# All GpSimd sums and products of a hybrid DeltaNet and pooling step issued on VectorE, with a new port rule in the kernel's scheduler

## The chip, the cores and the metric

The kernel runs on one core of one Trainium2 chip. The metric is the device time of one execution in microseconds. Before the change it is 2344.27 us, the median of three runs (2341.98 to 2349.40).

The core has five instruction queues that run beside each other, each in its own order: TensorE (PE in the profile; its weight loads are PEld), VectorE (DVE), ScalarE (ACT), GpSimd (POOL) and SyncE (SP), which issues the DMA transfers here. An instruction waits at the head of its queue until the semaphores of the instructions it depends on have come; what stands behind it waits too.

## The reference

One layer on 2048 prompt frames and 64 frames of a running stream, model width 1024, in float32:

```
h    = rmsnorm(x, norm1_w);  proj = h @ w_in          # q, k, v, z (4 heads x 128 each), a, b, pooling input
q,k,v = silu(conv4(qkv));  q,k = l2norm(q), l2norm(k)
# per head, chunks of tokens:  Lm = strict_lower((k*beta) k^T * gamma);  T = (I + Lm)^-1
# u = T (v*beta), w = T (k*beta*exp(G));  S carried from chunk to chunk;  o = q S + (q k^T * gamma) v_new
o    = rmsnorm(o) * silu(z)
pool = (sum of the last 2/4/8/16 frames / count - frame) @ pool_w * pool_scale
x    = x + concat(o, pool) @ w_out
h    = rmsnorm(x, norm2_w)
x    = x + (silu(h @ w_gate) * (h @ w_up)) @ w_down   # inner width 2816
y    = rmsnorm(x, normf_w)
```

The outputs are y of both streams and the new convolution, delta and pooling states.

## The kernel before

**Precision.** A large matmul is three: a float32 factor is split into a high part (ScalarE copies it to the matmul type fp32r) and a low part (VectorE subtracts the copy from the original), and high x high, high x low and low x high are added in PSUM. So each weight tile and each activation tile costs one ScalarE copy and one VectorE subtraction (`wsplit`, line 571; `split`, line 711).

**First part, up to about 948 us.** Four token blocks (576, 512, 512 and 512 tokens). Per block: the norm (`norm_stats`, `norm_apply`), the input projection (matmuls `pp`), the convolution and SiLU, and for each of 16 block-heads two `Front`s of two chunks. A `Front` (line 908) inverts a triangular 128x128 matrix in seven doubling levels: at each level `Um`, which is `U` times a mask, then fp16 matmuls `py`, a ScalarE copy `Yt`, fp16 matmuls `pt`, and an update of `TV` by VectorE. `Head` then walks through the chunks with the carried state. `pool_group` (line 1281) makes the window sums by doubling (`pw`). The output projection has the matmuls `pz`. The front's matmuls run in fp16 or plain float32 between the projections' fp32r ones.

**Second part, from about 948 us.** Three token blocks of 704, each in two halves of 352. For each of 22 inner tiles, `gate_up` (line 1561) makes the gate and the up projection as a 2x2 block product with seven instead of eight products (Strassen's scheme in Winograd's form): the seven products go into three PSUM accumulators, called px, py and pz here, 84 matmuls of 128x352 in all. Between the products the hurried instructions `g`, `u` and `hr` read those accumulators: before the last product can be added to px, VectorE must have made `u<-px,u`, so TensorE waits for it there. The down projection does the same for most groups (`down_strassen`, matmuls dx, dy, dz) and is plain for the rest (`down`, matmuls d). The sums and differences that the scheme needs are made of the weights (`prep_strassen`, line 624, tiles wr and wrS; `prep_down`, line 658, tiles wrdt, wrdl, wrda, wrdb) and of the activations (`factors`, line 1622, tiles q and hr; `stats2`, line 1356, tiles xt and xd). The gate and up weights are prepared in the first of the three blocks, stored, and mostly read back in the later ones.

**What sets the order.** The kernel first notes all operations in program order (`Machine.note`), and then plays them on a model of the five engines (`Machine.play`, line 237): each operation has a cost (`cost`, line 141), an occupancy `occ` of its engine and a latency `lat`, and each engine takes the ready operation of the lowest rank. Two plays are made; after the first, `deadlines` turns TensorE's order into due times, which are the ranks of the other engines in the second. The order of the second play is the order in which every queue is issued. All instructions are issued at line 206, so every row of the profile has that line; rows are told apart by tile names.

Around the change: the model knows that VectorE and GpSimd get in each other's way. An operation with `port` set is lengthened by what the other engine's last one still has to run, by no more than its own occupancy (line 361). GpSimd's operations all have it, VectorE's only with two inputs of the output's shape and none in PSUM. Operations that go to GpSimd before the change: the four sums of `prep_strassen` and of `prep_down`, the four of `factors` and of `stats2`, the running sums of squares of the norms (`rstd`, `last_norm`), the product in `norm_apply`, the `Um`, `Umf`, `Gst` operations and one `TV` of each `Front`, the pooling sums, the product with silu(z) in `Head.norm`, and the low parts of four of eight activation tiles in `load_h` (table `HPOOL`) - beside 193 small copies (2 to 15 elements a partition) and some memsets.

Of the kernel before, what the change touches and what calls it, by code (L numbers as in the profile page):

```python
# [19 lines left out]
P = 128  # L20
# [39 lines left out]
class Machine:  # L60
# [80 lines left out]
    def cost(self, op, name, out, ins):  # L141

        n = 1
        for d in out.shape[1:]:
            n *= d
        if op.eng == "tensor":
            dt = ins[0].dtype
            if name == "transpose":
                op.kind, op.ldw, op.occ = "f", 0.11, 0.109
            elif dt == F32:  # L150
                op.kind, op.ldw, op.occ = "f", 0.11, 0.012 + 1.651e-3 * n
            elif dt == F32R:
# [12 lines left out]
        if op.eng == "vector":
            op.lat = (0.215 if name == "scalar_tensor_tensor" else 0.15) + 1.045e-3 * n
            if name == "memset":
                op.lat = 0.14 + 0.5e-3 * n
            op.occ = op.lat - 0.083
            op.port = 1 if wide > 1 and not ps else 0  # L170
        elif op.eng == "scalar":
            op.lat = (0.16 if ps else 0.2) + 0.84e-3 * n + 0.095 * max(0, len(ins) - 1)
            op.occ = op.lat - 0.1
            if "accum_out" in op.call[2]:
                op.lat, op.occ = 0.6, 0.3
        else:
            op.port = 1
            if len(ins) > 1:
                op.lat = 0.05 + (2.45e-3 if n <= 512 else 1.92e-3) * n
            else:  # L180
                op.lat = 0.19 + 0.85e-3 * n
            op.occ = op.lat - 0.05

# [152 lines left out]
    def run(self, op, t):  # L336
        op.start = t
        if op.eng == "tensor":

            free, kind = self.free["tensor"], op.kind  # L340
            if self.last == kind and op.ready <= free:
                op.start = max(t, self.at + op.ldw)
            elif kind == "r":
                if op.ready <= free:
                    op.start = max(op.ready, free - (0.028 if self.last == "h" else 0.081))
                op.occ, op.lat = op.occ + 0.087, op.lat + 0.087
            elif self.last == "h":
                op.occ, op.lat = op.occ + 0.054, op.lat + 0.054
            else:
                op.occ, op.lat = op.occ + 0.02, op.lat + 0.02  # L350
            self.at, self.last = op.start, kind
            self.free["tensor"] = op.start + op.occ
        elif op.eng == "sync":
            self.free["sync"] = t + op.occ
            self.wire = max(self.wire, t + op.occ) + op.size / (400e3 if op.size > 300000 else 320e3)
            op.lat = self.wire + 1.35 - t
        else:
            if op.port:

                other = "gpsimd" if op.eng == "vector" else "vector"  # L360
                more = min(max(self.busy[other] - t, 0.0), op.occ)
                op.occ, op.lat = op.occ + more, op.lat + more
                self.busy[op.eng] = t + op.occ
            self.free[op.eng] = t + op.occ
# [31 lines left out]
def hybrid_kernel(ctx, tc, a, o):  # L396
# [173 lines left out]

    def wsplit(t, raw, n=512, eng=None):
        nc.scalar.copy(t[:, 0, :n], raw[:, :n])
        (eng or nc.vector).tensor_tensor(out=t[:, 1, :n], in0=raw[:, :n], in1=t[:, 0, :n].bitcast(F32), op=ALU.subtract)

    def prep():
# [31 lines left out]
        elif key[0] == "dn":  # L607
            _, m, f0, G = key
            raw, parts = (f() for f in wtiles("d", m % 2 == 0))
            nc.sync.dma_start(out=raw[:, : G * P], in_=a["wd"][m][:, f0 * P : (f0 + G) * P])  # L610
            wsplit(parts, raw, G * P, nc.vector)
        elif key[0] == "ds":
            parts = prep_down(*key[1:])
        else:
            parts = prep_strassen(key)
# [8 lines left out]
    def prep_strassen(key):  # L624
# [9 lines left out]
        if old:  # L634
            for i, nm in enumerate(FW):
                t[nm] = wtiles(nm, i % 2 == 1)[1]()
                if nm in gsd:
                    nc.sync.dma_start(out=flat(t[nm]), in_=gsd[nm][key[1]])
                else:
                    get(nm, nm)  # L640
                    wsplit(t[nm], raw[nm], 512, nc.vector)
            return t
        for nm, src in (("11", "11"), ("S1", "21"), ("22", "22"), ("12", "12")):
            get(nm, src)
        for nm in ("S3", "S2", "S4"):
            raw[nm] = wtiles(nm, True)[0]()
        gt = nc.gpsimd.tensor_tensor
        gt(out=raw["S3"], in0=raw["11"], in1=raw["S1"], op=ALU.subtract)
# [3 lines left out]
        for i, nm in enumerate(FW):  # L652
            t[nm] = wtiles(nm, i % 2 == 1)[1]()
            wsplit(t[nm], raw[nm], 512, nc.vector)
        due.append((key, [(gsd[nm][key[1]], t[nm]) for nm in FW if nm in gsd]))
        return t

    def prep_down(m, f0, G):
# [5 lines left out]
        s31, s24 = (wtiles(f"d{i}", True)[0]() for i in "ab")  # L664
        gt = nc.gpsimd.tensor_tensor
        left, right = slice(0, n), slice(n, 2 * n)
# [5 lines left out]
        for i, (nms, raw) in enumerate(((("11", "12"), top), (("S3", "S1"), s31), (("S2", "S4"), s24), (("22",), low[:, right]))):  # L672
            part = wtiles(f"d{nms[0]}", i % 2 == 1)[1]()
            wsplit(part, raw, n * len(nms), nc.vector)
            for j, nm in enumerate(nms):
# [86 lines left out]

    def rstd(tag, r, src, subs, pool, ttag, tbufs, eng):

        for lo, n in subs:
            rs = r[:, lo : lo + n]
            for k in range(KT):
# [3 lines left out]
                else:  # L771
                    sq = pool.tile([P, n], F32, tag=ttag, name=f"sq{k}{tag}{lo}", bufs=tbufs)
                    act(sq[:, :n], x, AF.Square)
                    eng.tensor_tensor(out=rs, in0=rs, in1=sq[:, :n], op=ALU.add)
                yield LAT_STAT
# [13 lines left out]
    def norm_stats(B):  # L789
# [8 lines left out]
        else:  # L798
            Chain(rstd(f"n1_{B.j}", B.r, stream_x(a["xT"], "xa", B.t0), [(0, B.NB)], gp, "ext", 4, nc.gpsimd))

    def norm_apply(B):
# [5 lines left out]
        for lo, n in S0 if B.j == 0 else [(0, B.NB)]:  # L807
            sl = slice(lo, lo + n)
            for k in range(KT):
# [5 lines left out]
                else:  # L815
                    t = src(k, lo, n)
                    nc.gpsimd.tensor_tensor(out=t, in0=t, in1=B.r[:, sl], op=ALU.mult)
                    act(h[:, 0, sl], t, AF.Copy, scale=w)
# [89 lines left out]
    class Front:  # L908
# [46 lines left out]
        def all(self):  # L955
# [42 lines left out]
            U = lev(F32, "Gst")  # L998
            nc.gpsimd.tensor_tensor(out=U, in0=Gam, in1=bc(ident, 2, C), op=ALU.subtract)
            yield LAT_G  # L1000
# [14 lines left out]
            for l in range(nlev):  # L1015
                Um = lev(F16, "Um", l, bufs=2)
                nc.gpsimd.tensor_tensor(out=Um, in0=U, in1=bc(lmask[:, l], 2, C), op=ALU.mult)
                py = self.ps(f"py{l}_{tag}")
                for c in range(2):
                    mm(py[:, c * C : (c + 1) * C], Um[:, c], id16 if l == 0 else TV[:, 0, c], start=True, stop=True)  # L1020
                if l == 0:
                    idb = bc(id16, 2, C)
                    TV = lev(F16, "TV", "", [P, 2, 2, C])
                    tt(TV[:, 0], idb, two(py), ALU.subtract)
                    nc.gpsimd.tensor_tensor(out=TV[:, 1], in0=idb, in1=Um, op=ALU.subtract)
                else:
# [16 lines left out]
            F0 = lev(F16, "Um", "f", bufs=2)  # L1043
            nc.gpsimd.tensor_tensor(out=F0, in0=bc(id16, 2, C), in1=T, op=ALU.subtract)
            pf = self.ps(f"pf_{tag}")
# [32 lines left out]
    class Head:  # L1078
# [11 lines left out]
        def norm(self, W, po, qsq):  # L1090
# [11 lines left out]
            stt(osq[:, :W], po[:, :W], onw, osq[:, :W], ALU.mult, ALU.mult)  # L1102
            nc.gpsimd.tensor_tensor(out=osq[:, :W], in0=osq[:, :W], in1=self.Yvz[:, 1, :W], op=ALU.mult)
            return osq
# [176 lines left out]
    def pool_group(B, g, pp):  # L1281
# [11 lines left out]
        while step < win:  # L1293
            nx = gp.tile([P, PX], F32, tag="pw", name=f"pw{j}_{g}_{step}", bufs=2)
            lo = 2 * step - 1
            nc.gpsimd.tensor_tensor(out=nx[:, lo:PW], in0=cur[:, lo:PW], in1=cur[:, lo - step : PW - step],
                                    op=ALU.add)
# [58 lines left out]
    def stats2(b, pool, tag, tbufs):  # L1356

        r = cpool.tile([P, TB2], F32, tag="r", name=f"r{b}")
        src = stream_x(x2d, f"xd{b}_", TB2 * b)
        yield from rstd(f"n2_{b}", r, src, SUBS2, pool, tag, tbufs, nc.gpsimd)  # L1360
        yield 4.0
        gt = nc.gpsimd.tensor_tensor

# [95 lines left out]
    def load_h(b, names):  # L1459
        for nm in names:  # L1460
            for k in range(4):
# [3 lines left out]
                nc.scalar.copy(t[:, 0], raw)  # L1465
                (nc.gpsimd if b and k in HPOOL else nc.vector).tensor_tensor(
                    out=t[:, 1], in0=raw, in1=t[:, 0].bitcast(F32), op=ALU.subtract)
# [58 lines left out]
    def last_norm(b, ys, i, done):  # L1526

        rf = tmp(f"rf{b}_{i}")
        for k in range(KT):
# [92 lines left out]
    def factors(b, f, u, v):  # L1622
# [231 lines left out]
```

## Time and profile before

| | |
|---|---|
| median of three runs | 2344.27 us |
| the profiled execution's own time | 2342.91 us |
| its span in the profile | 2341.1 us |
| PE busy | 2306.0 us, 99% |
| DVE busy | 1657.3 us, 71% |
| ACT busy | 1265.4 us, 54% |
| POOL busy | 1047.4 us, 45%, 1178 instructions |

Some 1.8 us of the execution lie outside the span. Busy time counts the stretches in which at least one instruction of the engine runs. Matmuls overlap each other: a 128x352 one shows some 320 ns from start to end, but in an unbroken run one starts every 159 ns, and that distance is what a matmul costs. The same holds on VectorE, where the next instruction starts a little before the end shown for the one ahead.

### The profile page before, as it was taken

The numbers are of one execution on the slowest core, as the hardware profiler recorded it, in microseconds if no ns is written. First come the engines' busy times: TensorE is split into PE (matmuls) and PEld (weight loads), VectorE is DVE, ScalarE is ACT, GpSimd is POOL, SyncE is SP. The second block draws the span as 40 slices with busy tenths as digits, with TensorE's granted clock in tenths as the row PEclk, the third lists the DMA queues.
The fourth block names the chain that finished last, engine by engine and source line by source line (L and its number), as shares of the span: only waits on it lengthen the run. The fifth ranks groups of instructions, "written<-read, shape, count | busy, mean of one in ns | idle before, by whom it ended". The sixth has DMA issues, their size and how long they took to land.

```text
span 2341.1 us, 41677 instructions
## 1 busy us (share of the span) xinstructions
PE 2306.0 (99%) x14729; PEld 2139.8 (91%) x14729; DVE 1657.3 (71%) x2946; ACT 1265.4 (54%) x2920; POOL 1047.4 (45%) x1178
## 2 busy tenths in 40 slices
PE   9999999999999999999999999999999999999998
PEld 8998798777777778999999999999999999999998
DVE  7998865784677785777698983776566757646466
ACT  7786755673658764655354564553433554424334
POOL 1658544663567670533355544452323653203212
PEclk9999999999999999999999999999999999999999
DMA  7665475546465667988686588877865697575763
GB/s 287 230 199 184 142 250 184 188 141 204 163 208 174 194 195 244 365 305 312 245 324 241 196 314 280 285 272 241 298 222 175 197 343 256 175 237 178 261 213 112
DMA packets 228386, 540.33 MB, mean 231 GB/s; under 512 B 28368, under 2 KB 86736, under 8 KB 228176
## 3 DMA queue, kind: packets, MB, share of 16 engines
q1 hardware_dynamic: 228176, 537.66, 67.3%
q8 instruction: 116, 1.90, 0.3%
q14 instruction: 94, 0.77, 0.1%
HBM read 389.15 MB, written 148.41 MB: 230 GB/s over the span
## 4 chain that ended last, share of the span: by engine, by line
PE 82%; DVE 8%; ACT 4%; DMA 2%; issue 2%; SPq 0%; POOL 0%; DVEq 0%; POOLq 0%; ACTq 0%
PE px L206 18%; PE pp L206 16%; PE pz L206 12%; PE py L206 8%; PE dx L206 7%; PE d L206 7%; PE dy L206 3%; PE pk_p L206 2%; PE pt_p L206 2%; PE dz L206 2%; DVE hq L206 1%; PE gr_p L206 1%; ACT hr L206 1%; PE py_p L206 1%; DVE wsS L206 1%
## 5 line engine op out<-in xcount | busy, mean ns | idle before, releaser
L206 PE MATMUL pp<-h,wsp 128*128 128x512 f32 (+1 forms) x2480 | 554.8, 364 | 0.4 <-DMA wsp<-wnd 0.4
L206 PEld LDWEIGHTS pp<-h,wsp 128*128 128x128 f32 x2480 | 400.0, 189 | 47.5 <-issue 1.2
L206 POOL TENSOR_TENSOR Um_p<-Gst_p,lmask 128x256 f16<-128x256 f32 x224 | 191.2, 865 | 102.6 <-PE py_p L206 64.1
L206 PE MATMUL pz<-op,wsp 128*128 128x512 f32 (+1 forms) x960 | 210.6, 362 | 0.0
L206 PEld LDWEIGHTS pz<-op,wsp 128*128 128x128 f32 x960 | 156.0, 188 | 18.9 <-issue 0.5
L206 PE MATMUL d<-h3l,wsd 128*128 128x352 f32 x1056 | 170.7, 322 | 1.0 <-DVE h3l L206 0.6
L206 PEld LDWEIGHTS d<-h3l,wsd 128*128 128x128 f32 x1056 | 168.5, 188 | 2.1 <-DVE h3l L206 1.2
L206 ACT COPY g<-px 128x352 f32<-128x352 f32 x132 | 59.4, 451 | 185.8 <-PE px L206 185.4
L206 ACT ACTIVATE hr<-g 128x352 f32<-128x352 f32 x132 | 65.7, 498 | 158.6 <-DVE g L206 158.3
L206 PE MATMUL px<-hBT,wsS 128*128 128x352 f32 x792 | 139.8, 325 | 7.4 <-ACT g L206 7.4
L206 PE MATMUL px<-hBT,ws 128*128 128x352 f32 x792 | 138.5, 323 | 8.7 <-DVE u L206 8.7
L206 PE MATMUL px<-hA,ws 128*128 128x352 f32 x792 | 140.4, 322 | 0.7 <-DVE ws L206 0.7
L206 PE MATMUL py<-hB,wsS 128*128 128x352 f32 x792 | 140.5, 322 | 0.0
L206 PE MATMUL pz<-hB,ws 128*128 128x352 f32 x792 | 138.5, 322 | 0.0
L206 PEld LDWEIGHTS px<-hBT,wsS 128*128 128x128 f32 x792 | 129.3, 190 | 9.7 <-ACT g L206 9.7
L206 PEld LDWEIGHTS px<-hBT,ws 128*128 128x128 f32 x792 | 127.9, 188 | 11.1 <-DVE u L206 10.9
L206 PE MATMUL px<-hA,wsS 128*128 128x352 f32 x792 | 137.6, 322 | 0.3 <-ACT g L206 0.3
L206 PE MATMUL py<-hA,wsS 128*128 128x352 f32 x792 | 137.8, 322 | 0.0
L206 PEld LDWEIGHTS px<-hA,ws 128*128 128x128 f32 x792 | 128.8, 188 | 1.1 <-DVE ws L206 1.0
L206 PEld LDWEIGHTS py<-hB,wsS 128*128 128x128 f32 x792 | 129.1, 188 | 0.0
L206 PEld LDWEIGHTS px<-hA,wsS 128*128 128x128 f32 x792 | 128.3, 188 | 0.8 <-ACT g L206 0.8
L206 PEld LDWEIGHTS py<-hA,wsS 128*128 128x128 f32 x792 | 128.5, 188 | 0.0
(700 smaller groups left out, 5565.4 us busy)
## 6 DMA issues: line engine op xcount, KB each, us to landing
wsS<-gS SPq DMA_DIRECT2D x176, 512.0 KB, 4.8
ws<-g SPq DMA_DIRECT2D x132, 512.0 KB, 4.7
wsp<-wnd SPq DMA_DIRECT2D x126, 512.0 KB, 3.3
gS<-wsS SPq DMA_DIRECT2D x88, 512.0 KB, 5.4
g<-ws SPq DMA_DIRECT2D x66, 512.0 KB, 5.3
wnd<-wsp SPq DMA_DIRECT2D x42, 512.0 KB, 4.9
xd<-x2d SPq DMA_DIRECT2D x96, 176.0 KB, 3.6
wr<-in_wg_dram SPq DMA_DIRECT2D x44, 256.0 KB, 3.9
```

Source lines behind the costliest of these rows:

```text
L206: getattr(getattr(self.nc, op.eng), name)(*args, **kw)
```

## The change

Every `tensor_tensor` of GpSimd is given to VectorE: 969 instructions. GpSimd keeps its small copies and memsets. The table `HPOOL` and the arguments that named an engine go. In the model, an operation on VectorE with no operand in PSUM now holds the port (with an offset, `port`, of 0.135 or 0.2 us), the waiting is no longer limited to the operation's own occupancy, the busy mark is the end of the latency instead of the occupancy, and some costs are refitted (`tensor_copy` on VectorE, GpSimd's products by type and size).

```diff
@@ Machine.cost
         if op.eng == "vector":
             op.lat = (0.215 if name == "scalar_tensor_tensor" else 0.15) + 1.045e-3 * n
-            if name == "memset":
+            if name in ("memset", "tensor_copy"):
                 op.lat = 0.14 + 0.5e-3 * n
             op.occ = op.lat - 0.083
-            op.port = 1 if wide > 1 and not ps else 0
+            if not ps:
+                op.port = 0.2 if name == "scalar_tensor_tensor" else 0.135
...
         else:
-            op.port = 1
-            if len(ins) > 1:
-                op.lat = 0.05 + (2.45e-3 if n <= 512 else 1.92e-3) * n
+            op.port = 0.14
+            if len(ins) < 2:
+                op.lat = 0.19 + 0.85e-3 * n
+            elif n > 512:
+                op.lat = 0.05 + 1.92e-3 * n
+            elif mybir.dt.size(out.dtype) < 4:
+                op.lat = 0.05 + 2.45e-3 * n
             else:
-                op.lat = 0.19 + 0.85e-3 * n
-            op.occ = op.lat - 0.05
+                op.lat = 0.16 + 2.23e-3 * n
+            op.occ = op.lat - 0.042
@@ Machine.run
-                more = min(max(self.busy[other] - t, 0.0), op.occ)
+                more = max(self.busy[other] - t - op.port, 0.0)
                 op.occ, op.lat = op.occ + more, op.lat + more
-                self.busy[op.eng] = t + op.occ
+                self.busy[op.eng] = t + op.lat
@@ prep_strassen, prep_down, stats2, factors
-        gt = nc.gpsimd.tensor_tensor
+        gt = tt
@@ rstd
-                    eng.tensor_tensor(out=rs, in0=rs, in1=sq[:, :n], op=ALU.add)
+                    tt(out=rs, in0=rs, in1=sq[:, :n], op=ALU.add)
@@ norm_apply
-                    nc.gpsimd.tensor_tensor(out=t, in0=t, in1=B.r[:, sl], op=ALU.mult)
+                    tt(out=t, in0=t, in1=B.r[:, sl], op=ALU.mult)
@@ Front.all
-            nc.gpsimd.tensor_tensor(out=U, in0=Gam, in1=bc(ident, 2, C), op=ALU.subtract)
+            tt(out=U, in0=Gam, in1=bc(ident, 2, C), op=ALU.subtract)
...
-                nc.gpsimd.tensor_tensor(out=Um, in0=U, in1=bc(lmask[:, l], 2, C), op=ALU.mult)
+                tt(out=Um, in0=U, in1=bc(lmask[:, l], 2, C), op=ALU.mult)
@@ load_h
-                (nc.gpsimd if b and k in HPOOL else nc.vector).tensor_tensor(
+                tt(
                     out=t[:, 1], in0=raw, in1=t[:, 0].bitcast(F32), op=ALU.subtract)
@@ last_norm
-                nc.gpsimd.tensor_tensor(out=rf, in0=rf, in1=sq, op=ALU.add)
+                tt(out=rf, in0=rf, in1=sq, op=ALU.add)
```

Two places in the queues, before and with the change.

VectorE in the second part, first token block, between inner tiles 13 and 14: hr is the gated product, hq and h the split factors of the down projection, q their sums, wsd and wsdS split down weights, wrda and wrdb their sums, g and u the hurried readers of PSUM. Before:

```order
L206 TENSOR_TENSOR hq_13_3465<-hr_12_3443,hq_13_3465 128x352
L206 TENSOR_TENSOR hq_13_3465<-hr_13_3458,hq_13_3465 128x352
L206 TENSOR_TENSOR hq_13_3465<-q_13_3468,hq_13_3465 128x352
L206 TENSOR_TENSOR hq_13_3465<-q_13_3467,hq_13_3465 128x352
L206 TENSOR_TENSOR g_0_14_3482<-pz_14_3481,g_0_14_3482 128x352
L206 TENSOR_TENSOR wsdS_156_3441<-wrdb_3438,wsdS_156_3441 128x512
L206 TENSOR_TENSOR h_13_3466<-q_13_3469,hq_13_3465 128x352
L206 TENSOR_TENSOR hr_14_3478<-hr_14_3478,g_0_14_3482 128x352
L206 TENSOR_TENSOR u_0_14_3483<-px_14_3479,u_0_14_3483 128x352
```

With the change:

```order
L211 TENSOR_TENSOR q_13_3469<-hr_13_3458,q_13_3468 128x352
L211 TENSOR_TENSOR g_0_14_3482<-pz_14_3481,g_0_14_3482 128x352
L211 TENSOR_TENSOR wrda_3452<-wrdt_3450,wrdl_3451 128x256
L211 TENSOR_TENSOR wrda_3452<-wrdl_3451 128x256
L211 TENSOR_TENSOR h_13_3466<-q_13_3469,hq_13_3465 128x352
L211 TENSOR_TENSOR wrdb_3453<-wrda_3452,wrdt_3450 128x256
L211 TENSOR_TENSOR wsdS_156_3441<-wrdb_3438,wsdS_156_3441 128x512
L211 TENSOR_TENSOR wrdb_3453<-wrdt_3450,wrdb_3453 128x256
L211 TENSOR_TENSOR wsdS_157_3455<-wrda_3452,wsdS_157_3455 128x512
L211 TENSOR_TENSOR hr_14_3478<-hr_14_3478,g_0_14_3482 128x352
L211 TENSOR_TENSOR u_0_14_3483<-px_14_3479,u_0_14_3483 128x352
```

Between g and u VectorE had three instructions before and has eight now: four of them (wrda and wrdb, twice each) were GpSimd's, and one more split (wsdS) has been drawn ahead.

The inversion of two fronts in block 0 (heads 1 and 2). On GpSimd before:

```order
L206 TENSOR_TENSOR Um_p_2_0_509<-Gst_p_2_0_474,lmask 128x256
L206 TENSOR_TENSOR Um_p_2_0_522<-Gst_p_2_0_474,lmask 128x256
L206 TENSOR_TENSOR TV_p_2_0_511<-id_162,Um_p_2_0_509 128x256
L206 TENSOR_TENSOR Um_p_1_1_559<-Gst_p_1_1_438,lmask 128x256
L206 TENSOR_TENSOR Um_p_2_0_531<-Gst_p_2_0_474,lmask 128x256
L206 TENSOR_TENSOR Um_p_2_0_556<-Gst_p_2_0_474,lmask 128x256
```

On VectorE with the change, at the same place of the same front:

```order
L211 TENSOR_TENSOR Um_p_2_0_509<-Gst_p_2_0_474,lmask 128x256
L211 TENSOR_TENSOR Um_p_2_0_522<-Gst_p_2_0_474,lmask 128x256
L211 TENSOR_TENSOR TV_p_1_1_458<-TV_p_1_1_458,pt_p_1_1_503 128x2x32x4
L211 TENSOR_TENSOR TV_p_2_0_511<-id_162,Um_p_2_0_509 128x256
L211 TENSOR_TENSOR osq_p_0__463<-osq_p_0__463,Yvz_0_168 128x512
L211 SCALAR_TENSOR_TENSOR Uhl_p_2_0_547<-Gst_p_2_0_474,Uhl_p_2_0_547 128x256
L211 TENSOR_TENSOR TV_p_2_0_511<-id_162,py_p_2_0_510 128x256
L211 TENSOR_TENSOR Um_p_2_0_531<-Gst_p_2_0_474,lmask 128x256
```

The mask products and the product with silu(z) now stand in one queue with the updates of TV that read PSUM.

More of the change, by code (lines that the diff above doesn't have):

```diff
@@ L569, in wtiles, with wsplit @@
                 lambda: pool.tile([P, 2, 512], F32R, tag="wsp" + x, name=f"ws{nm}_{at}", bufs=4))
-    def wsplit(t, raw, n=512, eng=None):
+    def wsplit(t, raw, n=512):
         nc.scalar.copy(t[:, 0, :n], raw[:, :n])
-        (eng or nc.vector).tensor_tensor(out=t[:, 1, :n], in0=raw[:, :n], in1=t[:, 0, :n].bitcast(F32), op=ALU.subtract)
+        tt(out=t[:, 1, :n], in0=raw[:, :n], in1=t[:, 0, :n].bitcast(F32), op=ALU.subtract)
     def prep():
@@ L610, in prep @@
             nc.sync.dma_start(out=raw[:, : G * P], in_=a["wd"][m][:, f0 * P : (f0 + G) * P])
-            wsplit(parts, raw, G * P, nc.vector)
+            wsplit(parts, raw, G * P)
         elif key[0] == "ds":
@@ L640, in prep_strassen @@
                     get(nm, nm)
-                    wsplit(t[nm], raw[nm], 512, nc.vector)
+                    wsplit(t[nm], raw[nm], 512)
             return t
@@ L653, in prep_strassen @@
             t[nm] = wtiles(nm, i % 2 == 1)[1]()
-            wsplit(t[nm], raw[nm], 512, nc.vector)
+            wsplit(t[nm], raw[nm], 512)
         due.append((key, [(gsd[nm][key[1]], t[nm]) for nm in FW if nm in gsd]))
@@ L664, in prep_down @@
         s31, s24 = (wtiles(f"d{i}", True)[0]() for i in "ab")
-        gt = nc.gpsimd.tensor_tensor
+        gt = tt
         left, right = slice(0, n), slice(n, 2 * n)
@@ L673, in prep_down @@
             part = wtiles(f"d{nms[0]}", i % 2 == 1)[1]()
-            wsplit(part, raw, n * len(nms), nc.vector)
+            wsplit(part, raw, n * len(nms))
             for j, nm in enumerate(nms):
@@ L761, in colsum, with rstd @@
         mm(ps, onesr, lo, start=False, stop=True)
-    def rstd(tag, r, src, subs, pool, ttag, tbufs, eng):
+    def rstd(tag, r, src, subs, pool, ttag, tbufs):
         for lo, n in subs:
@@ L798, in norm_stats @@
         else:
-            Chain(rstd(f"n1_{B.j}", B.r, stream_x(a["xT"], "xa", B.t0), [(0, B.NB)], gp, "ext", 4, nc.gpsimd))
+            Chain(rstd(f"n1_{B.j}", B.r, stream_x(a["xT"], "xa", B.t0), [(0, B.NB)], gp, "ext", 4))
     def norm_apply(B):
@@ L1024, in all @@
                     tt(TV[:, 0], idb, two(py), ALU.subtract)
-                    nc.gpsimd.tensor_tensor(out=TV[:, 1], in0=idb, in1=Um, op=ALU.subtract)
+                    tt(out=TV[:, 1], in0=idb, in1=Um, op=ALU.subtract)
                 else:
@@ L1043, in all @@
             F0 = lev(F16, "Um", "f", bufs=2)
-            nc.gpsimd.tensor_tensor(out=F0, in0=bc(id16, 2, C), in1=T, op=ALU.subtract)
+            tt(out=F0, in0=bc(id16, 2, C), in1=T, op=ALU.subtract)
             pf = self.ps(f"pf_{tag}")
@@ L1102, in norm @@
             stt(osq[:, :W], po[:, :W], onw, osq[:, :W], ALU.mult, ALU.mult)
-            nc.gpsimd.tensor_tensor(out=osq[:, :W], in0=osq[:, :W], in1=self.Yvz[:, 1, :W], op=ALU.mult)
+            tt(out=osq[:, :W], in0=osq[:, :W], in1=self.Yvz[:, 1, :W], op=ALU.mult)
             return osq
@@ L1295, in pool_group @@
             lo = 2 * step - 1
-            nc.gpsimd.tensor_tensor(out=nx[:, lo:PW], in0=cur[:, lo:PW], in1=cur[:, lo - step : PW - step],
+            tt(out=nx[:, lo:PW], in0=cur[:, lo:PW], in1=cur[:, lo - step : PW - step],
                                     op=ALU.add)
@@ L1359, in stats2 @@
         src = stream_x(x2d, f"xd{b}_", TB2 * b)
-        yield from rstd(f"n2_{b}", r, src, SUBS2, pool, tag, tbufs, nc.gpsimd)
+        yield from rstd(f"n2_{b}", r, src, SUBS2, pool, tag, tbufs)
         yield 4.0
-        gt = nc.gpsimd.tensor_tensor
+        gt = tt
         def put(nm, k, t):
@@ L1514, in final_norm @@
             src = lambda k, *_: ys[k][:, i]
-            yield from rstd(f"nf{b}_{i}_", rf, src, [(0, N2)], f2, "t", TB, nc.gpsimd)
+            yield from rstd(f"nf{b}_{i}_", rf, src, [(0, N2)], f2, "t", TB)
             for k in range(KT):
@@ L1631, in split @@
             tt(lo, x, hi.bitcast(F32), ALU.subtract)
-        gt = nc.gpsimd.tensor_tensor
+        gt = tt
         t3, t2, t4 = (tmp(f"q{i}{b}_{f}") for i in (3, 2, 4))
@@ L1738 @@
 HOT_ROWS = BOOST
-HPOOL = (0, 1, 2, 3)
 LAT_LOAD = 0.6
```

## The prediction

> **What bounds the kernel now.** First the page: busy shares, the slices and the chain of waits.
>
> ```profile
> PE 2306.0 (99%) x14729; PEld 2139.8 (91%) x14729; DVE 1657.3 (71%) x2946; ACT 1265.4 (54%) x2920; POOL 1047.4 (45%) x1178
> PEclk9999999999999999999999999999999999999999
> PE 82%; DVE 8%; ACT 4%; DMA 2%; issue 2%; SPq 0%; POOL 0%; DVEq 0%; POOLq 0%; ACTq 0%
> ```
>
> TensorE is busy 99% of the span at full clock, and GpSimd has 0% of the chain. No TensorE work is removed, so the change can only win back stretches in which TensorE idles, and lose by making new ones. How large are they? The windows by stage (columns: stretch, its length, then busy us and count of PE, PEld, DVE, ACT, POOL, the granted clock, DMA share, GB/s):
>
> ```profile
> 60.00:300.00 240.00, 238.24 (x1838) 210.50 (x1837) 220.24 (x448) 180.72 (x470) 158.35 (x217) 1.00 0.56 189
> 300.00:930.00 630.00, 628.34 (x3967) 506.17 (x3966) 430.48 (x799) 381.32 (x979) 338.65 (x420) 1.00 0.59 193
> 950.00:1400.00 450.00, 434.83 (x2690) 430.52 (x2689) 366.77 (x548) 243.34 (x496) 211.71 (x172) 1.00 0.79 289
> 1400.00:2320.00 920.00, 915.50 (x5704) 910.80 (x5703) 567.38 (x991) 400.71 (x837) 316.64 (x328) 1.00 0.71 236
> 990.00:1000.00 10.00, 6.43 (x41) 6.14 (x40) 8.47 (x10) 4.33 (x11) 5.44 (x4) 1.00 0.84 315
> 1000.00:1010.00 10.00, 10.00 (x54) 10.00 (x55) 7.29 (x14) 8.02 (x18) 4.06 (x3) 0.83 0.98 349
> 1200.00:1260.00 60.00, 55.17 (x339) 54.01 (x339) 56.31 (x84) 32.37 (x65) 35.05 (x32) 1.00 0.63 226
> ```
>
> TensorE idles 450 - 434.83 = 15.2 us in the first block of the second part, 4.5 us in the two others, 1.8 + 1.7 = 3.4 us in the first part. After the longest idle stretch (3.6 us at 990) the granted clock falls to 0.83 for 10 us. In an unbroken run
>
> ```profile
> 1035.70 30.57 PE d L206 x192
> 908.27 40.16 PE pz L206 x177
> ```
>
> a 128x352 matmul costs 30.57/192 = 0.159 us (a 128x512 one 0.227), so 10 us hold about 63, and 54 are 1.5 us short. What may be won there is 15.2 + 1.5 + 4.5 + 3.4 = 24.6 us, about 1% of the span.
>
> Who is late? TensorE's waits name two:
>
> ```profile
> PE px L206 <- DVE u L206: 8.7, 6, 2.8
> PE px L206 <- ACT g L206: 7.7, 9, 3.6
> ```
>
> The timeline of VectorE and GpSimd ahead of one of the longest, between inner tiles 13 and 14, shows why:
>
> ```profile
> 1227.29 1.33 POOL L206 TENSOR_TENSOR q<-hr,hr 128x352 f32<-128x352 f32 x1 [0.46 <-DVE hr L206]
> 1231.24 1.27 POOL L206 TENSOR_TENSOR q<-hr,q 128x352 f32<-128x352 f32 x1
> 1234.33 1.02 POOL L206 TENSOR_TENSOR wrdb<-wrda,wrdt 128x256 f32<-128x256 f32 x1
> ...
> 1227.73 1.43 DVE L206 TENSOR_TENSOR wsd<-wrdt,wsd 128x512 fp32r<-128x512 f32 x1
> 1229.09 1.27 DVE L206 TENSOR_TENSOR hq<-hr,hq 128x352 fp32r<-128x352 f32 x1
> 1230.28 1.43 DVE L206 TENSOR_TENSOR ws<-wr,ws 128x512 fp32r<-128x512 f32 x1
> 1231.63 1.16 DVE L206 TENSOR_TENSOR wsd<-wrdl,wsd 128x256 fp32r<-128x256 f32 x1
> 1232.72 2.03 DVE L206 TENSOR_TENSOR hq<-hr,hq 128x352 fp32r<-128x352 f32 x2
> 1234.68 1.49 DVE L206 TENSOR_TENSOR hq<-q,hq 128x352 fp32r<-128x352 f32 x2
> 1236.09 0.51 DVE L206 TENSOR_TENSOR g<-pz,g 128x352 f32<-128x352 f32 x1
> 1236.53 0.67 DVE L206 TENSOR_TENSOR wsdS<-wrdb,wsdS 128x512 fp32r<-128x512 f32 x1
> 1237.12 0.51 DVE L206 TENSOR_TENSOR h<-q,hq 128x352 fp32r<-128x352 f32 x1
> 1238.32 0.97 DVE L206 TENSOR_TENSOR hr<-hr,g 128x352 f32<-128x352 f32 x1 [0.68 <-ACT hr L206]
> 1239.77 1.54 PE L206 MATMUL px<-hBT,ws 128*128 128x352 f32 x8 [2.45 <-DVE u L206]
> ```
>
> Beside a busy GpSimd, hq takes 1.27 us and ws 1.43; once GpSimd pauses, instructions of the same sizes take 0.51 and 0.67. So g comes late, the sigmoid behind it too, hr stands 0.68 us at the head of VectorE's queue waiting for it, and u, which TensorE wants, stands behind hr.
>
> **The change part by part.** The groups by shape give the prices (busy us, mean ns of one, idle before):
>
> ```profile
> L206 POOL TENSOR_TENSOR Um_p<-Gst_p,lmask 128x256 f16<-128x256 f32 x224 | 191.2, 865 | 102.6 <-PE py_p L206 64.1 <-DVE Gst_p L206 27.9 <-DVE kn_p L206 4.4
> L206 POOL TENSOR_TENSOR wrS<-wr,wrS 128x512 f32<-128x512 f32 x44 | 63.7, 1447 | 139.4 <-DMA wrS<-in_wu_dram 49.3 <-DMA xh<-hpd 27.4 <-DMA wr<-in_wg_dram 18.7
> L206 DVE TENSOR_TENSOR wsS<-wrS,wsS 128x512 fp32r<-128x512 f32 x88 | 82.6, 948 | 10.9 <-ACT wsS L206 10.5
> L206 DVE TENSOR_TENSOR hq<-hr,hq 128x352 fp32r<-128x352 f32 x88 | 71.5, 822 | 3.9 <-ACT hq L206 3.1
> L206 DVE TENSOR_TENSOR ws<-wr,ws 128x512 fp32r<-128x512 f32 x66 | 60.3, 914 | 4.4 <-ACT ws L206 4.1
> L206 DVE TENSOR_TENSOR u<-px,u 128x352 f32<-128x352 f32 x66 | 34.4, 522 | 55.3 <-PE px L206 55.2
> ```
>
> *Added to VectorE.* Instruction to instruction, a 128x352 product takes 1236.53 - 1236.09 = 0.44 us and a 128x512 one 1237.12 - 1236.53 = 0.59; the same slope gives 0.35 for 128x256. Against GpSimd's means that is 0.35/0.865 and 0.59/1.447, both 0.4. GpSimd's 1047 us hold some 70 of copies and memsets, which stay, so VectorE gets about 977 x 0.4 = 390 us.
>
> *Given back to VectorE.* With 0.67 and 0.51 us as undisturbed, wsS is stretched by 88 x 0.28 = 24 us, hq by 88 x 0.31 = 27 and ws by 66 x 0.24 = 16: 67 us of 214, or 31%. All groups of the view taken in this way give about 250, the upper bound; these three alone, 67, are the lower. I take 200, nearer the full count, less what overlaps at both ends of an instruction. VectorE then has 1657 + 390 - 200 = about 1850 us, 79% (1800 to 1980, 77 to 85%). On the average it fits; what counts is where.
>
> *Second part, first block (term A).* In the hot stretch above, VectorE ran nine instructions from 1227.7 to 1236.5, g included, and GpSimd seven products and sums beside them (the first at 1227.29, the last at 1234.33). At undisturbed distances the nine are two of 512, six of 352 and one of 256 = 4.2 us, and the seven four of 352 and three of 256 = 2.8: 7.0 us in one queue instead of 8.8 in two, which is 1.8 of the 2.45 us that TensorE lost. Beside that, g and u are hurried and now stand among short instructions, and the model has the lengths that will come, so fewer orders should go wrong. u itself reads PSUM and takes 522 ns either way; only the queue ahead of it shortens. Of 15.2 us I take 10 back (0 to 15.2), and the 1.5 us of clock with the gap at 990 that causes them: -11.5.
>
> A rule speaks against that. The Trainium skill, page "SBUF — State Buffer", section "Who interferes with whom", says that GpSimd's SBUF port pair is also VectorE's second one, that a VectorE instruction with two SBUF inputs and a GpSimd one that reads SBUF fully block each other, and that one SBUF input does not conflict. By it g, u and y, which have one, were never held themselves, in agreement with 522 ns, so the change frees nothing of what TensorE waits for directly and only sets more work in front; by that alone term A would be 0.
>
> *Two later blocks (term B)*: same mechanism, fewer weights to split; 2 of 4.5 us: -2.
>
> *First part (term C).* In 60:300 VectorE is busy 220 of 240 us. It gets some 142 us of GpSimd's tensor work x 0.4 = 57, and gives back 57 x 200/390 = 29 (37 by 250): 240 to 248 us of 240. So block 0 is just full. TensorE can run on with projections while a front waits, and VectorE has room in 300:930 (430 + 135 - 69 = 496 of 630), so most of a delay is made up. I take +2 net of the 3.4 that could be won (bounds -3.4 and +28, the last if the 20 us of idle that VectorE has now are all waits for others: 248 + 20 - 240).
>
> *TensorE's order (term D).* Switching between number formats costs time:
>
> ```profile
> 500.36 1.87 PE L206 MATMUL pp<-h,wsp 128*128 128x512 f32 x7
> 502.07 0.28 PE L206 MATMUL pt_p<-Yt_p,TV_p 128*128 128x128 f16 x2
> ```
>
> Seven take 502.07 - 500.36 = 1.71 us, 0.12 more than 7 x 0.227. The new queue has about 400 such runs where there were 420: -2 (0 to -2.5).
>
> *Tail (term E).* The last norm's sum goes over GpSimd:
>
> ```profile
> 2331.52 0.86 PE L206 MATMUL rpnf<-rf,ones 128*128 128x352 f32 x2 [0.68 <-POOL rf L206]
> ```
>
> On VectorE it is half as long: -0.7.
>
> *New waits (term F).* The first instruction on a freshly loaded weight stood on GpSimd, where waiting for a DMA (the 49.3 and 18.7 us in the wrS row) held nobody. Now it stands in VectorE's queue, with g and u behind it. ScalarE reads the same loads already and shows how well the order foresees them:
>
> ```profile
> ACT hB L206 <- DMA xh<-hpd: 16.9, 10, 4.1
> ACT ws L206 <- DMA wr<-in_wg_dram: 4.2, 2, 2.8
> ```
>
> Small, but not nothing: +3 (0 to +7.7, what TensorE lost behind ScalarE's g). The port rule itself changes little: GpSimd keeps 193 copies of at most 15 elements.
>
> *Sum:* -11.5 - 2 + 2 - 2 - 0.7 + 3 = -11.2 us. The profiled execution had 2342.9 us (span 2341.1 and 1.8 around it), so 2331.7; the median of the runs is 1.4 above it: **2333 us**.
>
> **Rivals.**
>
> 1. *The hurried instructions gain nothing (rule above).* For it: in 1200:1260 VectorE is busy 56.3 of 60 us, and what the change adds (35.05 x 0.4 = 14) is about what it frees there (31% of at most 56 = 17). The stalls stay; D, E remain: 2341.5, no change. Against it: the 1.27 and 1.43 us right ahead of the late g.
> 2. *VectorE becomes the bound of block 0 - slower.* One queue carries the convolution, the evictions of block 0, the inversions and now the mask products. If its waits for TensorE and ScalarE stay as they are, the stage 60:300 grows by 28 us, and with A, B, D, E and F still -13 the time is 2344.3 + 15 = 2359. It decides if TensorE loses over 20 us there. Against: TensorE's order in the new queue has the heads of block 0 no later among the projections than before, and the overflow can run into 300:930.
> 3. *The order foresees nearly everything:* A, B, C at their bounds, no F: -16.7 - 4.5 - 3.4 - 2.5 - 1 = -28, 2316.
>
> **How the numbers follow.** Forecast 0.50, rival 1 0.24, rival 2 0.18, rival 3 0.08. The range 2317 to 2353 holds the forecast, rival 1 and the milder half of rival 2. This kernel's runs can tell 0.3%, 7 us. Faster by more: the forecast and rival 3, 0.58; within it: rival 1, 0.24; slower: rival 2, 0.18.
>
> **What would show it.** A: hq, ws and wsS at 0.51 to 0.69 us, TensorE's wait for u under 3 us, idle in 950:1400 near 5, no slice of clock under 1 at 1000. C: VectorE over 95% busy in 60:300, TensorE's idle there under 6 us. F: DVE waits for DMA of 10 us or more, none on the chain for long. VectorE's total near 1850 us; over 1950, and I have the stretching wrong. The prediction falls if TensorE idles over 10 us ahead of 300, or if px waits for u as long as now.

## The result, and the profile after

The changed kernel takes **2306.19 us** (median of five runs, 2305.14 to 2306.44); the kernel before, run beside it, 2344.86 (five runs, 2341.98 to 2349.40). The ratio is 0.983 (95% interval 0.982 to 0.985): 38.7 us less, where 11 were forecast, and below the low end of the range, 2317. The direction was right and, in the second part, so was the mechanism; the size was not, and for the first part no gain had been forecast (terms C and D, +2 and -2). The experiments ask why.

The page of the changed kernel, the rows that answer to those shown of before:

```profile
span 2304.7 us, 41103 instructions
PE 2293.5 (100%) x14729; PEld 2137.4 (93%) x14729; DVE 1765.3 (77%) x3915; ACT 1267.2 (55%) x2920; POOL 75.9 (3%) x209
PEclk9999999999999999999999999999999999999999
PE 98%; DMA 1%; DVE 0%; SPq 0%; ACT 0%; issue 0%; DVEq 0%; ACTq 0%
```

The same 14729 matmuls, and the chain of waits is now TensorE for 98% instead of 82. VectorE took over 969 instructions and is busy only 108 us longer. The windows by stage (stretch, length, busy us and count of PE, PEld, DVE, ACT, POOL, granted clock, DMA share, GB/s); the second part begins some 8 us earlier, so its stretches are shifted by that:

```profile
60.00:300.00 240.00, 240.00 (x1884) 214.25 (x1883) 232.09 (x597) 179.60 (x475) 28.28 (x69) 1.00 0.58 194
300.00:930.00 630.00, 629.98 (x3951) 507.21 (x3951) 482.32 (x1115) 385.15 (x982) 38.85 (x106) 1.00 0.60 195
942.00:1392.00 450.00, 450.00 (x2820) 450.00 (x2820) 382.77 (x750) 252.66 (x513) 0.00 (x0) 1.00 0.82 301
1392.00:2280.00 888.00, 887.90 (x5553) 886.79 (x5552) 596.15 (x1282) 392.23 (x819) 0.00 (x0) 1.00 0.71 238
```

TensorE idles for at most 0.1 us in any of them. All its waits that the view lists:

```profile
PE rpn L211 <- ACT sq4n L211: 1.2, 1, 1.2
PE idle L211 <- DVE chist L211: 1.1, 1, 1.1
PE rpnf L211 <- ACT sq7nf L211: 0.5, 1, 0.5
```

Neither u nor g is among them any more. The groups by shape (busy us, mean ns of one, idle before):

```profile
L211 DVE TENSOR_TENSOR Um_p<-Gst_p,lmask 128x256 f16<-128x256 f32 x224 | 91.3, 417 | 11.1 <-PE py_p L211 11.0
L211 DVE TENSOR_TENSOR wrS<-wr,wrS 128x512 f32<-128x512 f32 x44 | 30.1, 684 | 0.8 <-DMA wrS<-in_wu_dram 0.7
L211 DVE TENSOR_TENSOR wsS<-wrS,wsS 128x512 fp32r<-128x512 f32 x88 | 60.0, 686 | 9.9 <-ACT wsS L211 9.1
L211 DVE TENSOR_TENSOR hq<-hr,hq 128x352 fp32r<-128x352 f32 x88 | 45.1, 519 | 1.1 <-ACT hq L211 1.1
L211 DVE TENSOR_TENSOR ws<-wr,ws 128x512 fp32r<-128x512 f32 x66 | 45.2, 685 | 3.2 <-ACT ws L211 2.9
L211 DVE TENSOR_TENSOR u<-px,u 128x352 f32<-128x352 f32 x66 | 34.5, 523 | 40.4 <-PE px L211 40.2
```

wsS falls from 948 to 686 ns, hq from 822 to 519, ws from 914 to 685; u, which reads one operand from PSUM, stays at 523. In the place of the prediction's timeline, between inner tiles 13 and 14, VectorE now runs

```profile
1210.49 0.95 DVE L211 TENSOR_TENSOR hq<-hr,hq 128x352 fp32r<-128x352 f32 x2
...
1212.57 0.52 DVE L211 TENSOR_TENSOR q<-hr,q 128x352 f32<-128x352 f32 x1
1213.00 0.52 DVE L211 TENSOR_TENSOR g<-pz,g 128x352 f32<-128x352 f32 x1
1213.43 0.42 DVE L211 TENSOR_TENSOR wrda<-wrdt,wrdl 128x256 f32<-128x256 f32 x1
...
1214.87 0.68 DVE L211 TENSOR_TENSOR wsdS<-wrdb,wsdS 128x512 fp32r<-128x512 f32 x1
```

**Where the time went, by stage.** The first and the last px matmul of the first of its four products bound the second part (ns minimum/median/maximum, first and last start), before and after:

```profile
L206 PE MATMUL px<-hA,ws x792: 318/322/426, 948.3 to 2287.3; 128*128 128x352 f32 x198
```

```profile
L211 PE MATMUL px<-hA,ws x792: 317/322/432, 940.1 to 2250.9; 128*128 128x352 f32 x198
```

The first part is 948.3 - 940.1 = 8.2 us shorter; the stretch of 1339.0 us has become 1310.8, 28.2 less; what follows the last px start is 53.8 us in both (2341.1 - 2287.3 and 2304.7 - 2250.9). 8.2 + 28.2 is the whole difference of the spans, 36.4.

### The profile page after: what moved, and what is told of

Its sections match the earlier page's. It is cut to its first block, busy times and chain, and to the rows that moved or that the text cites. A ratio compares the mean times of both kernels' runs of the same rounds, so it can differ in the third digit from the quotient of the medians.

```text
span 2304.7 us, 41103 instructions
## 1 busy us (share of the span) xinstructions
PE 2293.5 (100%) x14729; PEld 2137.4 (93%) x14729; DVE 1765.3 (77%) x3915; ACT 1267.2 (55%) x2920; POOL 75.9 (3%) x209
## 4 chain that ended last, share of the span: by engine, by line
PE 98%; DMA 1%; DVE 0%; SPq 0%; ACT 0%; issue 0%; DVEq 0%; ACTq 0%
PE px L211 22%; PE pp L211 21%; PE pz L211 13%; PE py L211 11%; PE d L211 7%; PE dx L211 7%; PE dy L211 4%; PE pk_p L211 2%; PE pt_p L211 2%; PE dz L211 2%; PE gr_p L211 1%; PE py_p L211 1%; PE px_p L211 1%; PE rpn L211 0%; DMA x<-in_xT_dram 0%; PE gb_p L211 0%
## 5 line engine op out<-in xcount | busy, mean ns | idle before, releaser
L211 PEld LDWEIGHTS pz<-op,wsp 128*128 128x128 f32 x960 | 156.6, 188 | 19.7 <-issue 0.5
L211 PEld LDWEIGHTS pz<-hB,ws 128*128 128x128 f32 x792 | 128.6, 188 | 0.0
```

Of the source, the lines that this page charges most:

```text
L211: getattr(getattr(self.nc, op.eng), name)(*args, **kw)
```

## Experiments

Nine kernels; all times are medians, each with its ratio to the kernel before that was run beside it (2344.3 to 2345.8 us for the nine). "Second part" is the stretch from the first to the last px start, as above; the last two columns are from the profiled executions.

| kernel | us | ratio (95%) | first px at | second part |
|---|---|---|---|---|
| before | 2344.86 | | 948.3 | 1339.0 |
| the change | 2306.19 | 0.983 (0.982 to 0.985) | 940.1 | 1310.8 |
| model_only | 2324.13 | 0.992 (0.990 to 0.993) | 944.2 | 1324.8 |
| move_only | 2310.30 | 0.986 (0.984 to 0.987) | 943.8 | 1310.5 |
| front_on_gpsimd | 2312.32 | 0.987 (0.985 to 0.988) | 945.6 | 1310.9 |
| second_on_gpsimd | 2318.54 | 0.990 (0.988 to 0.991) | 940.7 | 1321.1 |
| side_reads | 2367.46 | 1.009 (1.008 to 1.011) | 939.7 | 1371.3 |
| side_reads_known | 2334.23 | 0.995 (0.994 to 0.997) | 940.0 | 1336.9 |
| side_writes | 2307.07 | 0.984 (0.982 to 0.985) | 940.1 | 1310.7 |
| side_on_vector | 2318.96 | 0.989 (0.987 to 0.991) | 940.0 | 1323.4 |
| no_gpsimd_copies | 2310.59 | 0.985 (0.983 to 0.987) | 944.7 | 1310.0 |

### The two halves of the change

**model_only**: before, with the new costs and the new port rule in the model; GpSimd keeps its sums.

```diff
-                more = min(max(self.busy[other] - t, 0.0), op.occ)
+                more = max(self.busy[other] - t - op.port, 0.0)
                 op.occ, op.lat = op.occ + more, op.lat + more
-                self.busy[op.eng] = t + op.occ
+                self.busy[op.eng] = t + op.lat
```

> The kernel before with the new costs and the new port rule in the scheduler; GpSimd keeps all 969 sums and products. Theory 1 (VectorE is held at the port while GpSimd reads SBUF; knowing it does not shorten anything): VectorE's groups stay stretched (wsS near 0.95 us, hq near 0.82), the order improves a little, 2335 to 2343 us. Theory 2 (the loss before was a wrong order, since the model took VectorE's instructions too short): most of the 38 us comes, 2310 to 2325 us.

**move_only**: the changed kernel with the old costs and the old rule (the same lines the other way round).

> The changed kernel with the old costs and the old port rule in the scheduler; VectorE does the sums. Theory 1: GpSimd is nearly empty, so the rule has nothing to act on; 2306 us within 4. Theory 2: without the new rule the order stays worse, 2320 us or more.

Groups, windows from the first px start and waits of model_only:

```profile
L211 DVE TENSOR_TENSOR wsS<-wrS,wsS 128x512 fp32r<-128x512 f32 x88 | 86.0, 986 | 11.2 <-ACT wsS L211 10.5
L211 DVE TENSOR_TENSOR hq<-hr,hq 128x352 fp32r<-128x352 f32 x88 | 69.9, 802 | 6.5 <-ACT hq L211 5.7
```

```profile
944.20:1394.20 450.00, 444.99 (x2763) 442.28 (x2762) 377.73 (x557) 248.59 (x506) 228.71 (x180) 1.00 0.81 294
1394.20:2274.20 880.00, 878.00 (x5472) 873.97 (x5471) 546.15 (x952) 382.29 (x800) 304.39 (x313) 1.00 0.72 242
```

```profile
PE px L211 <- ACT g L211: 4.0, 4, 2.0
PE px L211 <- DVE u L211: 0.4, 2, 0.3
```

VectorE's instructions are as stretched as before (986 and 802 ns), and yet 20 us of the 38 are won (18.3 between the profiled executions: 4.1 in the first part and 14.2 in the second): the order alone does that, and TensorE's wait for u has fallen from 8.7 us to 0.4. So the time is the second theory's, the lengths are the first one's. move_only wins 34 us and misses its first theory narrowly (4.1 us above the change, where 4 were allowed); its second part (1310.5) is as short as that of the full change. So in the second part the move takes all that any variant won, with either model, and with GpSimd kept the better model finds half of it. How the other half divides between the stretching and the longer way over GpSimd (a 128x352 sum q took 1.33 us there in the prediction's timeline, 0.52 on VectorE) was not separated. The two don't add up in the second part (14.2 and 28.5 against 28.2): both cure the same late u and g. In the first part they do: 4.1 + 4.5 against 8.2.

### Which part's sums

**front_on_gpsimd**: the changed kernel; the first part's sums (norm, `Um`, `Umf`, `Gst`, `TV`, pooling, silu(z)) go back to GpSimd. **second_on_gpsimd**: those of the second part go back (`gt`, the norms, `HPOOL`).

```diff
-                tt(out=Um, in0=U, in1=bc(lmask[:, l], 2, C), op=ALU.mult)
+                nc.gpsimd.tensor_tensor(out=Um, in0=U, in1=bc(lmask[:, l], 2, C), op=ALU.mult)
```

> The changed kernel, but the first part's sums and products (Um, Umf, Gst, TV, pooling, silu product, norms of blocks 1 to 3) are GpSimd's again; the second part's stay on VectorE. Theory 1 (stretching costs where it happens): the first matmul px starts near 948 us as before (940 with the change), the second part is as with the change, 2314 us in all. Rival (the first part's fronts were held by the latency of GpSimd's Um, not by the port): also near 948, but with VectorE's groups Yqk and wsp unstretched. A gain below 2306 would mean that VectorE is too full in block 0.

> The changed kernel, but the second part's sums (weights' and activations' Strassen sums, norms, half of the low parts in two blocks) are GpSimd's again; the first part's stay on VectorE. Theory 1: px starts near 940 us, the second part loses about 28 us again less what the new rule orders better, 2325 to 2335 us. Theory 2 (order): 2306 to 2315 us.

The window 60:300 of front_on_gpsimd, then the first 450 us of the second part of second_on_gpsimd:

```profile
60.00:300.00 240.00, 237.98 (x1830) 208.72 (x1829) 220.57 (x444) 177.93 (x467) 159.54 (x212) 1.00 0.57 187
```

```profile
940.70:1390.70 450.00, 447.26 (x2785) 444.56 (x2784) 368.84 (x558) 247.58 (x504) 229.23 (x183) 1.00 0.81 297
```

The parts are separate: front_on_gpsimd loses 5.5 us in the first and none in the second, second_on_gpsimd 10.3 in the second and 0.6 in the first. front_on_gpsimd came out near its first theory, and the rival's sign is missing: Yqk at 949 ns and wsp at 831 are as stretched as before (943 and 840; with the change 747 and 684). Whether GpSimd's latency adds to that stays open. second_on_gpsimd, at 2318.5, lies between the ranges of its two theories. In the window 60:300 TensorE starts 1830 matmuls with the sums on GpSimd and 1884 with them on VectorE, although VectorE is at 97% there.

### What costs the time: the port, the reads, or the order

Four kernels add useless work to the changed kernel's second part, twice for each inner tile, behind g; each batch waits for a tiny ScalarE copy of g. **side_reads** gives GpSimd five 128x256 sums of two SBUF inputs each time, and the model is told that they hold no port; **side_reads_known** is the same with the rule in force; **side_writes** has ten memsets of 128x256 in place of the five sums; **side_on_vector** puts four such sums on VectorE.

```diff
+        nc.scalar.copy(q[:, 0:1], x[:, 0:1])
+        for _ in range(5):
+            nc.gpsimd.tensor_tensor(out=so[:, :256], in0=q, in1=q, op=ALU.add)
...
+            if out.tensor.name.startswith("side"):
+                op.port = 0
```

> The changed kernel, and in the second part GpSimd runs 660 sums of its own (128x256, both inputs in SBUF, five at a time, twice per inner tile) whose results nobody uses and nobody waits for; one tiny ScalarE copy paces each five. The scheduler isn't told that they hold VectorE. Theory 1 (the port): VectorE's wsS, ws and hq are stretched again (wsS from 0.69 to 0.85 us or more) and the second part loses 10 us or more, 2316 to 2335 us. Theory 2 (what the move saved is the way over GpSimd, its latency and its waits): no work lies on that way, so 2306 to 2310 us and unstretched groups.

> The same side sums, but with the new port rule applied to them, so that the scheduler plans with VectorE held. Theory 1: stretched as in the run before, but the order gives way, about half of that loss (as model_only against before): 2310 to 2322 us. Theory 2: no difference from the run before.

> The same place and pace, but GpSimd fills the tile with ones instead (1320 memsets of 128x256, no SBUF read), busy about as long. Theory 1 with the port taken by reads alone (as the Trainium skill, page SBUF - State Buffer, section Who interferes with whom, has it): nothing is stretched, 2306 to 2310 us. If any GpSimd work holds VectorE: stretched, as side_reads.

> The changed kernel with 528 such side sums (four at a time) on VectorE itself, about 177 us more work: in the second part's first block VectorE would go from 384 to some 440 of 450 us. If a full VectorE costs TensorE time (rival 2 of the prediction): 2312 us or more, loss in that block. If the order keeps the urgent ones ahead up to the brim: 2306 to 2311 us.

side_reads, its added group, the stretched ones, the wait and the timeline behind one batch:

```profile
L213 POOL TENSOR_TENSOR side<-sides 128x256 f32<-128x256 f32 x660 | 510.6, 774 | 971.9 <-ACT sides L213 802.0 <-DMA gS<-wsS 125.3
L213 DVE TENSOR_TENSOR wsS<-wrS,wsS 128x512 fp32r<-128x512 f32 x88 | 70.9, 809 | 3.6 <-ACT wsS L213 3.0
L213 DVE TENSOR_TENSOR u<-px,u 128x352 f32<-128x352 f32 x66 | 34.2, 517 | 28.9 <-PE px L213 28.8
```

```profile
PE px L213 <- DVE u L213: 28.9, 18, 4.7
```

```profile
1229.05 4.10 POOL L213 TENSOR_TENSOR side<-sides 128x256 f32<-128x256 f32 x5 [6.19 <-ACT sides L213]
1229.18 0.93 DVE L213 TENSOR_TENSOR q<-hr,hr 128x352 f32<-128x352 f32 x1
1230.04 1.78 DVE L213 TENSOR_TENSOR hq<-hr,hq 128x352 fp32r<-128x352 f32 x2
...
1233.46 0.41 DVE L213 TENSOR_TENSOR wsd<-wrdl,wsd 128x256 fp32r<-128x256 f32 x1
```

Two hq side by side take 1.78 us while the five sums run, against 0.95 in the changed kernel; as soon as they end, lengths are the bare ones again (wsd 0.41). So 511 us of GpSimd sums, placed blindly behind g, cost 61 us, more than the 29 at most of the first theory and over twice what the second part of before lost, where GpSimd worked about as long (210 + 312 us, in the windows of before further down). With the rule in force the same sums cost 28 us (2334, above the forecast 2310 to 2322), at nearly the same stretching (wsS 786 ns instead of 809). In both, a part of the loss is TensorE's clock: granted at 0.66 in 980:990 and at 0.83 in 1240:1250, 1330:1340 and 1588:1598 of side_reads, which is 8.5 us at most, and at 0.83 and 0.53 in 1220:1230 and 1309:1320 of side_reads_known, 7 us at most. The wait for u that heads the list of side_reads is not at its head here:

```profile
L211 DVE TENSOR_TENSOR wsS<-wrS,wsS 128x512 fp32r<-128x512 f32 x88 | 68.5, 786 | 8.0 <-ACT wsS L211 7.4
```

```profile
PE dy L211 <- DVE wsdS L211: 2.8, 2, 1.5
PE px L211 <- ACT g L211: 2.4, 4, 0.9
```

Between the two only the model's rule for these sums differs, and with it the order. side_writes, whose GpSimd runs 410 us of memsets, is the changed kernel to within 0.9 us, with wsS at its bare length:

```profile
L213 POOL MEMSET sides<- 128x256 f32 x1320 | 410.4, 313 | 1009.8 <-ACT sides L213 942.5
L213 DVE TENSOR_TENSOR wsS<-wrS,wsS 128x512 fp32r<-128x512 f32 x88 | 60.1, 687 | 10.7 <-ACT wsS L213 9.8
```

It has the same copies on ScalarE at the same places as side_reads, and TensorE's order, by tile names, is the same at 14577 of 14729 places, so what costs the time there is that GpSimd sums two SBUF inputs instead of only writing. A memset is also shorter than a sum (313 against 774 ns); that was not varied apart. On VectorE itself 528 such sums cost 12.8 us:

```profile
L211 DVE TENSOR_TENSOR side<-sides 128x256 f32<-128x256 f32 x528 | 223.0, 422 | 55.9 <-ACT sides L211 45.3
```

```profile
940.00:1390.00 450.00, 446.78 (x2772) 442.02 (x2771) 429.80 (x898) 249.63 (x542) 0.00 (x0) 1.00 0.80 293
```

That is 0.024 us a sum, against 28/660 = 0.042 on GpSimd with the model told and 61/660 = 0.093 without. VectorE is at 430 of 450 us here; the changed kernel with its 383 was not at its limit.

### Is anything left

**no_gpsimd_copies**: the changed kernel, with GpSimd's remaining copies and memsets on VectorE too.

```diff
-            nc.gpsimd.tensor_copy(ext[:, 0:3], chist[:, m, :])
+            nc.vector.tensor_copy(ext[:, 0:3], chist[:, m, :])
```

> The changed kernel, with the rest of GpSimd's work (209 small copies and memsets, 75.9 us) moved to VectorE as well. Theory (TensorE has no lost time left in the stages): TensorE is busy 240.00 of 240 us in the window 60:300 and 450 of 450 in the first block of the second part, so there is nothing left to win; 2306, within 3 us, ratio to before 0.983 to 0.985, while VectorE's busy time rises by some 20 to 45 us and GpSimd's falls to under 5. Rival (the copies at the heads of the convolution's chains, 404 ns each on GpSimd, still delay the first part's fronts, and copies of one input need no shared port): the first part gets 3 to 6 us shorter, 2300 to 2303. If it is slower by over 5 us, VectorE's queue in 60:300 (232 of 240 us busy) had no room for even that.

```profile
60.00:300.00 240.00, 239.03 (x1866) 212.59 (x1865) 236.13 (x666) 179.35 (x474) 0.00 (x0) 1.00 0.56 191
```

The second part is as short as it gets (1310.0); the first is 4.6 us longer. Both theories missed: nothing was won, and the added copies did harm. In 60:300, where VectorE was at 232 of 240 us, it is now at 236, and TensorE starts 18 matmuls fewer. So the first part may be near the edge on VectorE's side; whether the room or the place of the copies in VectorE's queue did it was not separated. No variant that was run beats the change.

## Why the prediction was right or wrong

**The step that failed is the ceiling: "what may be won there is 15.2 + 1.5 + 4.5 + 3.4 = 24.6 us".** The change won 36.4 between the profiled executions, 25.2 more than the forecast -11.2: 14.7 of that in terms A and B, 8.2 in C and D, 2.3 in E and F. Idle time in the busy view isn't the time that TensorE loses: a matmul shows 322 ns, and one starts every 159, so the first 0.16 us of every gap still counts as busy, and a shorter gap isn't seen. What a stretch loses is told by its count of matmuls. With the same start (the first px) and the same length, before:

```profile
948.30:1398.30 450.00, 434.99 (x2691) 430.68 (x2689) 366.77 (x549) 244.18 (x498) 210.01 (x171) 1.00 0.79 289
1398.30:2278.30 880.00, 875.34 (x5453) 871.06 (x5454) 544.30 (x949) 377.47 (x792) 311.93 (x322) 1.00 0.72 242
```

and after:

```profile
940.10:1390.10 450.00, 450.00 (x2820) 450.00 (x2819) 383.73 (x752) 252.86 (x513) 0.00 (x0) 1.00 0.83 302
1390.10:2270.10 880.00, 879.90 (x5503) 878.79 (x5502) 588.94 (x1270) 387.74 (x810) 0.00 (x0) 1.00 0.72 241
```

129 matmuls fewer in the first 450 us and 50 in the next 880, at 450/2820 = 0.160 us each: 20.6 + 8.0 = 28.6 us, and 28.2 were measured. The same reckoning fits the runs on the way: model_only lacks 57 and 31, 14.0 us, and is 14.0 us longer than the change. The view had shown 15.2 + 1.5 + 4.5 = 21.2. The count could have been read ahead of the result, from the 2690 matmuls in 950:1400 against 450/0.159 = 2830 at the unbroken pace. Counted in the trace of before, from each matmul's start to the next, these 1330 us hold 25 gaps that the view shows, at 19.7 us, and that cost 23.8 beyond the pace of 0.16; 36 distances over 0.2 us in which the view shows no gap, 3.7; and the slice of lower clock, 1.6. That is 29.1 us, against 1.0 with the change. So the hidden heads of gaps are about half of what the idle time lacks, and the delays too short to be seen are the other half. Two windows can be compared by count only where the work is of one kind: in 300:930 the faster kernel starts 3951 matmuls and the slower 3967, since other work falls into that window.

The busy share of the weight loads (PEld) would have told it: in the prediction's rows they lack 450 - 430.52 = 19.5 and 920 - 910.80 = 9.2 us. The Trainium skill, page "Perfetto Trace Analysis", section "Identifying the Most-Contended Engine", says just that: matmul busy time is no good measure of how near TensorE is to its limit, and the busy share of weight loads is one of the two to use instead. The traces agree in the second part, 28.7 us by the weight loads against 28.2 measured. In the first part the share tells nothing of the kind: in 60:300 the loads are busy 210.50 us of 240 before and still only 214.25 with the change, where TensorE is busy throughout.

**Terms A and B** were also taken too low inside their ceiling: -13.5 of 21.2, against -28.2 measured, nearly all of the loss. The mechanism is as described: hq, ws and wsS at 0.51 to 0.69 us, no wait for u, no idle time in the first block, no slice of lower clock. The assumption that a third of the gaps would stay had no row behind it; model_only shows such a remainder, 14 us, and there the stretching has stayed too.

**Given back to VectorE.** 65 us of the three named groups (67 worked out). In all, 969 instructions at 390 us raised the busy time by 108, so some 282 came back or weren't needed: more than the 200 taken and than the 250 called the upper bound. Taken group by group over the shapes that both kernels have on VectorE in equal number, the means times the counts are 275 us shorter, so the stretching is nearly all of it. Some 8 us of the difference are in 64 products of two fp16 inputs:

```profile
L211 DVE TENSOR_TENSOR TV_p<-id,Um_p 128x256 f16<-128x256 f16 x32 | 9.1, 283 | 0.0
L211 DVE TENSOR_TENSOR Umf_p<-id,TV_p 128x256 f16<-128x256 f16 x32 | 9.0, 284 | 0.1
```

283 ns instead of the 417 of `Um`, a product of this size with a float32 input. VectorE's total, 1765 us, is below the bounds of 1800 to 1980.

**Term C has the wrong sign**: +2 forecast, -8.2 measured. VectorE was to be full in 60:300, with 240 to 248 us; it has 232, since more came back than was reckoned. The ceiling's error is in it too: 3.4 us of idle time were visible there, and over twice that was won. The sums' move is 4.5 us of it with the old model and 5.5 with the new one (front_on_gpsimd), the model alone 4.1; how that splits among inversions, norms, pooling and refitted costs was not tried. "The port rule itself changes little" was off by some 4 us as well: move_only, with the old rule and costs, is 4.1 us slower than the change, 3.7 of them in the first part.

**Term D** (format switches, -2) was not measured apart; it may be part of the 8.2 of the first part. **Term E** (-0.7 in the tail): the wait for rf, 0.7 us, is now one for ScalarE's sq7nf, 0.5, and the tail is 53.8 us in both: 0. **Term F** (+3): the waits came, and cost nothing. The largest of VectorE's:

```profile
DVE xt L211 <- DMA hpd<-xd: 6.5, 2, 3.7
DVE wrda L211 <- DMA wrdl<-in_wd_dram: 2.9, 2, 2.2
DVE wrS L211 <- DMA wr<-in_wu_dram: 2.1, 2, 1.5
```

They add up to over the 10 us that were named as a sign, but TensorE's list shows no wait behind any of them.

**Rival 1** (the hurried instructions gain nothing) fell, though its rule stands. By the Trainium skill, page "SBUF — State Buffer", section "Who interferes with whom", a GpSimd instruction that only writes doesn't hold a VectorE one with two SBUF inputs, and one SBUF input doesn't conflict. side_writes agrees with the first (687 ns), u with the second, at 517 to 523 ns in before, in the change and in side_reads. The inference failed: u was never held itself, but what stood ahead of it was, and in the old order that made it late (model_only, as stretched in a better order, waits 0.4 us for it). **Rival 2** (VectorE as the bound of block 0) fell for the change, and no_gpsimd_copies, with 4 us more of VectorE in 60:300, may show its edge. **Rival 3** (the order foresees nearly everything, 2316) was the nearest; it took A, B and C at their bounds and still fell 10 us short, since those bounds were the idle times of the busy view.

## What to carry to other kernels

Read what a pipelined engine loses from the number of its instructions in equal stretches of like work, against its unbroken pace; the idle time of its busy view is only a lower bound, here 20 of 28 us. Where an engine off the critical path slows an engine that feeds it, the price is what stands in the queue ahead of the few hurried instructions, and an order that knows the slowing recovered half of it here (14 of 28 us). And a slower helper engine whose reads stretch the engine that it helps carries less than it seems to: the 969 instructions, about 390 us of VectorE's time, cost it only 108 us of busy time when they were moved back, in a kernel where it had 684 to spare.

## What the runs showed of the hardware that was not expected

- GpSimd's memsets left VectorE alone: 410 us of them changed the time by 0.9 us (side_writes, wsS at 687 ns), where 511 us of two-input sums cost 61 (side_reads, wsS at 809).
- The sums cost more when the order doesn't know of them than their own stretching explains: 61 us against 28, with wsS at 809 and 786 ns and VectorE busy 1874 and 1861 us.
- With VectorE at 236 instead of 232 of 240 us in 60:300 the first part was 4.6 us longer (no_gpsimd_copies); whether the lack of room did it is not shown.
